# Three value products in other PSUM banks, the down unit's low parts last, and one weight split moved behind an addition

## The chip, the core and the metric

The kernel runs on one core of one Trainium2 chip. The metric is the device time of one execution in microseconds (us), the median of the runs shown. Matrix products run on TensorE (PE in the rows; PEld is its weight load), elementwise work on VectorE (DVE), ScalarE (ACT) and GpSimd (POOL), and transfers between the chip's memory and the core are started from SyncE's queue (SP), from POOL's and from ACT's.

## What is computed

One inference step of a two-layer decoder over 512 prompt tokens and 8 sample tokens (520 columns), with 1024 features. Layer 0 mixes tokens by sliding-window attention, layer 1 by gated linear attention (GLA). Behind each mixer comes a normalisation, then a gated feed-forward with a causal convolution, then another normalisation:

```python
def conv_ffn(x, buf, w_up, conv_w, conv_b, w_down):
    T = x.shape[1]
    h = x @ w_up
    a, u = h[..., :D_FF], h[..., D_FF:]          # gate branch, value branch; D_FF = 2816
    ap = jnp.concatenate([buf.astype(a.dtype), a], axis=1)
    c = conv_b + sum(conv_w[j] * ap[:, j:j + T] for j in range(CONV_W))
    y = (jax.nn.gelu(c, approximate=False) * u) @ w_down
    return y, ap[:, T:]
...
        xp = layer_norm(ALPHA * xp + mp, ln_mix_g[i], ln_mix_b[i])
        fp, cp = conv_ffn(xp, buf0, ffn_w_up[i], ffn_conv_w[i], ffn_conv_b[i], ffn_w_down[i])
        xp = layer_norm(ALPHA * xp + fp, ln_ffn_g[i], ln_ffn_b[i])
```

## The kernel before

All activations are held transposed, features on the 128 partitions and tokens along the row, in two groups of columns: group a has tokens 0 to 255, group b tokens 256 to 511 and the 8 sample tokens (264 columns). Every 32-bit operand of a matrix product is split into a high and a low part that TensorE reads in a single pass each. A product is then three matmuls for every 128 features: high weight by high input (L236), high weight by low input (L238) and low weight by high input (L240, or L243 where the lows come last). In the rows `xh`/`xl` are the high and low parts of the input, `wh`/`wl` those of a weight; `xs_a` and `hs_a` hold both parts of group a.

A weight is a tile of 128 x 1024, loaded into `raw` from SP's queue. ScalarE copies it to `wh` (L194, L313). The low part is made in one of two ways: VectorE subtracts (`wl<-raw,wh`, L200, L314), or ScalarE writes the negated high part to `wl` (L205) and a transfer from POOL's queue adds the weight from memory onto it (`low_by_dma`, L206). The up weights of the plain blocks, and those of the down units in `ffn_down2`, take the second way.

The first four of the 22 blocks of 128 feed-forward features are "plain": for each group a gate product (`ffn_gate`), then a value product (`ffn_value`), whose result VectorE multiplies by the gate (`hprod`, L817). I write g2a for the gate of block 2, group a, and v2a for its value. They begin while the normalisation of the mixer is still at work on group b. The products go into a ring of four PSUM banks named accp (`ACCS = 4`); the normalisation has banks of its own, `tp`, `pv` and two of `sc`, handed out by `mtile`. VectorE's eight `x_b<-x_b,par,pv` (L435) are the last to read the norm's `pv` for group b; behind them ScalarE makes `xh_b` (L436).

The other 18 blocks are "pairs" (`ffn_pair`): seven half products per block, in double banks widep0 to widep2 and two single ones (`onep`). ScalarE copies onep to `nv` (L852) and VectorE adds it to a wide bank (`merged<-widep,nv`, L844). Between the pairs stand down units. `ffn_down2` handles the first parts of the down product: for two column blocks s, and for each feature block, high-high, high-low and low-high (L919, L920, L921). The last part is `ffn_down`: four heads and four further products, each of which goes to `ln_chunk`, where VectorE adds it to x (L335) and TensorE forms a first sum of the norm from column block 0 (`sc<-x_a,ones_a`, L341). The weights of this last part are let loose (`release`) in a chosen order: `kinds` lists six of them.

The code is written in an order of tasks, but the order on each engine is set when the program is built: a list scheduler with its own estimates places every instruction, and then it is fixed. `issue_after(ins)` forbids placing an instruction ahead of another. So a change of three lines can move rows in stages whose code it doesn't touch.

Of the kernel before, what the change touches and what calls it, by code (L numbers as in the profile page):

```python
# [11 lines left out]
F32 = mybir.dt.float32  # L12
# [3 lines left out]
ALU = mybir.AluOpType  # L16
# [4 lines left out]
P = 128  # L21
# [64 lines left out]
def in_turn(rows):  # L86

    return rows.rearrange("p t j -> p j t")
# [10 lines left out]
class Net:  # L99
# [124 lines left out]
    def product(self, g, u, rh, rl):  # L224
        nc = self.nc
        h, l = self.w[u]
        nt = self.units[u][1]

        tail = u in self.phases[2::3] or g.i and u in self.phases[2:4]
        behind = self.units[u][2] == self.ffn_down and g.i == 0 or g.i == 0 and nt == KD and not tail and any(e < u < e + LOWS for e in (*self.phases[2:4], *self.phases[5:6]))  # L230
        ps = self.acc.tile([P, 512], F32, name="accp")
        o = ps[:, :g.n].rearrange("p (j t) -> p j t", t=2)
        for k in range(nt):
            ks = slice(k * P, (k + 1) * P)
            xh, xl = in_turn(rh[:, k]), in_turn(rl[:, k])
            nc.tensor.matmul(o, h[:, ks], xh, start=k == 0, stop=False)  # L236
            if not tail:
                nc.tensor.matmul(o, h[:, ks], xl, start=False, stop=False)  # L238
            if not behind:
                nc.tensor.matmul(o, l[:, ks], xh, start=False, stop=not tail and k == nt - 1)  # L240
        for k in range(nt) if tail or behind else ():
            w, r = (h, rl) if tail else (l, rh)
            nc.tensor.matmul(o, w[:, k * P:(k + 1) * P], in_turn(r[:, k]), start=False, stop=k == nt - 1)  # L243
        self.final = self.nc.cur_bb.bb.instructions[-1]
        return ps[:, :g.n]
# [80 lines left out]
    def ln_chunk(self, g, m, ps, scaled, last=False):  # L326


        nc, n, x = self.nc, g.n, g.x
        t = lambda name: self.ln.tile([P, g.n], F32, name=f"{name}_{g.name}")  # L330
        c = lambda name, b=1: self.ln.tile([P, NT - 256], F32, name=name, bufs=b)[:, :n]
        if m:
            yield 0
        if scaled:
            nc.vector.scalar_tensor_tensor(x[:, m], x[:, m], self.back[:, m:m + 1], ps, op0=ALU.add, op1=ALU.add)  # L335
        else:
            nc.vector.scalar_tensor_tensor(x[:, m], x[:, m], ALPHA, ps, op0=ALU.mult, op1=ALU.add)
        if m == 0:
            yield 1
            mp = self.mtile("sc")[:, :n]  # L340
            nc.tensor.matmul(mp, self.ones_a, x[:, 0], start=True, stop=True)  # L341
            sb = c("sb")
            nc.scalar.activation(sb, mp, AF.Copy, scale=float(KD))
            sa = sb
            if not scaled:
                sa = c("sa")
                nc.scalar.activation(sa, mp, AF.Copy, scale=KD / ALPHA)
            for i in range(KD):
                eng = nc.gpsimd if i else nc.vector
                eng.tensor_tensor(x[:, i], x[:, i], sa if i else sb, op=ALU.subtract)  # L350
            g.s2 = t("s2")
            nc.scalar.activation(g.s2, x[:, 0], AF.Square)
            return
        q = c("sq", 2)
        sq = nc.scalar.activation(q, x[:, m], AF.Square)
        if m == 6 and g.i == 0:
            with self.tc.issue_after(sq.ins):
                nc.scalar.preload_act_table_set("natural_log_exp_and_others")
        if last and m == KD - 1:

            g.q = q
            return
        if m == 1:
            g.s1 = t("s1")

        p1, p2 = (KD - 1, KD - 1) if g.i and not last else (0, S2P)
        (nc.gpsimd if m < p1 else nc.vector).tensor_tensor(g.s1, x[:, 0] if m == 1 else g.s1, x[:, m], op=ALU.add)
        (nc.gpsimd if m < p2 else nc.vector).tensor_tensor(g.s2, g.s2, q, op=ALU.add)
# [452 lines left out]
    def ffn_pair(self, u, layer, j, q):  # L821


        nc, W = self.nc, self.w[u]
# [18 lines left out]
        n, m = a.n, b.n  # L843
# [3 lines left out]
        g, h = M[:, 0], M[:, 1, 2:]  # L847
# [38 lines left out]
        if j == NF - 1:  # L886
            kinds, self.held = self.held, None
            done = [next(x for x in reversed(nc.cur_bb.bb.instructions) if x.engine == engine)
                    for engine in (mybir.EngineType.Activation, mybir.EngineType.DVE)]
            with self.tc.issue_after(summed.ins):  # L890
                self.release()
                self.release(kinds[0])
            with self.tc.issue_after(done[0]), self.tc.issue_after(done[1]):
                for kind in kinds[1:]:
                    self.release(kind)
            nc.scalar.dma_start(out=self.O["conv_p"][layer], in_=self.nconv_p)
            nc.scalar.dma_start(out=self.O["conv_s"][layer], in_=self.nconv_s)
            for cm in (self.cp_cm, self.pp_cm, self.fp_cm):
                self.close(cm)
            self.close_psum()  # L900
            self.open_acc()

    def ffn_down2(self, u, layer, part, i):


        nc = self.nc
        h, l = self.w[u]
        j0, j1 = FF_PARTS[part]
        nk = j1 - j0
        ms = KD // nk  # L910
        for g, m in ((g, ms * i + m) for g in self.groups for m in range(0, ms, 2)):
            ps, n = self.wide(), g.n
            for s in range(2):
                o = ps[:, s, :n].rearrange("p (j t) -> p j t", t=2)
                for k in range(nk):
                    t, q = (m % ms + s) * nk + k, self.place(j0 + k)
                    ks = slice(t * P, t * P + P)
                    rh, rl = in_turn(g.hh[:, q]), in_turn(g.hl[:, q])
                    nc.tensor.matmul(o, h[:, ks], rh, start=k == 0, stop=False)  # L919
                    nc.tensor.matmul(o, h[:, ks], rl, start=False, stop=False)  # L920
                    self.final = nc.tensor.matmul(o, l[:, ks], rh, start=False, stop=k == nk - 1).ins  # L921
            x = g.x[:, m:m + 2]
            if part == 0:
                nc.vector.scalar_tensor_tensor(x, x, ALPHA, ps[:, :, :n], op0=ALU.mult, op1=ALU.add)
            else:
                nc.vector.tensor_tensor(x, x, ps[:, :, :n], op=ALU.add)
        self.release()
# [565 lines left out]
```

## Time and profile before

| | us |
|---|---|
| median of three runs | 1099.32 |
| lowest, highest | 1099.08, 1100.93 |
| profiled execution | 1098.55 |
| its span, first to last instruction | 1096.6 |
| TensorE busy in it | 1058.9 (97%) |
| VectorE, ScalarE, POOL busy | 882.0, 663.1, 303.1 |
| mean granted TensorE clock | 0.994 of full speed |

In a row of the timeline the first number is the start in us from the span's start, the second how long it was busy; then engine, line, operation, output and inputs, and the count where equal instructions are gathered. In brackets stands the idle time ahead of it and what ended that. Matmuls overlap: at full clock one starts about every 112 ns though each is 280 long, so a gap is read from start to start. In a row of windows stand the stretch, its length, the busy time of PE, PEld, DVE, ACT and POOL with counts, the granted clock, the share of the transfer engines and GB/s.

The plain blocks of layer 0 lie at about 170 to 214 us, those of layer 1 at about 745 to 790; the pairs at 225 to 455 and 802 to 1035; the last down parts at about 470 and 1047; the GLA stage at 520 to 740.

### The profile page before, as it was taken

To read this page: it belongs to the slowest core of one execution; us is meant where nothing else is said; L and a number is where in the kernel's file an instruction comes from. 1 tells how busy PE (TensorE), PEld (TensorE's weight loads), DVE (VectorE), ACT (ScalarE), POOL (GpSimd) and SP (SyncE) were. 2 spreads that over 40 slices of the span, in tenths; PEclk is the share of its full clock that TensorE was granted. 3 is DMA by queue.
4 is the path that set the end of the run, shared out by engine and by line. 5 is a ranking of instruction groups with operands and counts; after the bars stand their busy time and mean duration, and the time that the engine had idled before them with its cause. 6 is when DMAs were issued, how large, how long until landed. Compare 5 with 4: busy or idle time off the path is not lost.

```text
span 1096.6 us, 23781 instructions
## 1 busy us (share of the span) xinstructions
PE 1058.9 (97%) x9174; PEld 1031.2 (94%) x9174; DVE 882.0 (80%) x1797; ACT 663.1 (60%) x1308; POOL 303.1 (28%) x512
## 2 busy tenths in 40 slices
PE   8999999999999999999899999999999999999996
PEld 8997899999999999999799899899999999999995
DVE  7897668988778878978667678778988788888975
ACT  5677667766655665547545456458776655655643
POOL 4576562221111110274111100362221111110163
PEclk9999999999999999999999999999999999999998
DMA  7554048587777774437224364558588777774412
GB/s 233 147 173 125 21 128 207 135 215 191 180 177 178 176 174 116 124 130 204 66 74 145 115 185 136 164 170 215 134 205 197 180 174 177 175 185 116 116 66 79
DMA packets 65472, 167.44 MB, mean 153 GB/s; under 512 B 8104, under 2 KB 28624, under 8 KB 65360
## 3 DMA queue, kind: packets, MB, share of 16 engines
q1 hardware_dynamic: 50960, 119.47, 33.8%
q0 software_dynamic: 12240, 44.57, 23.1%
q10 hardware_dynamic: 2160, 1.89, 0.5%
q8 instruction: 72, 1.18, 0.4%
q14 instruction: 40, 0.33, 0.1%
HBM read 153.24 MB, written 8.47 MB: 147 GB/s over the span
## 4 chain that ended last, share of the span: by engine, by line
PE 66%; DVE 13%; DMA 10%; ACT 5%; issue 5%; SPq 1%; POOL 0%; DVEq 0%; ACTq 0%; POOLq 0%
PE widep L308 8%; PE widep L310 8%; PE widep L309 8%; PE accp L236 6%; PE accp L238 6%; PE accp L240 6%; PE widep L921 5%; PE widep L920 5%; PE widep L919 5%; DMA vb<-dv 2%; DMA wl<-in_w_up 2%; DVE wl L200 2%; PE onep L310 1%; PE onep L309 1%; PE onep L308 1%
## 5 line engine op out<-in xcount | busy, mean ns | idle before, releaser
L313 ACT ACTIVATE wh<-raw 128x1024 fp32r<-128x1024 f32 x72 | 76.2, 1061 | 98.7 <-PE widep L920 57.3
L194 ACT ACTIVATE wh<-raw 128x1024 fp32r<-128x1024 f32 (+1 forms) x92 | 96.0, 1047 | 52.3 <-PE accp L238 19.4
L309 PE MATMUL widep<-tl,wh 128*128 128x264 f32 (+1 forms) x432 | 119.1, 276 | 0.0
L310 PE MATMUL widep<-th,wl 128*128 128x264 f32 (+1 forms) x432 | 119.1, 276 | 0.0
L308 PE MATMUL widep<-th,wh 128*128 128x264 f32 (+1 forms) x432 | 119.1, 276 | 0.0
L236 PE MATMUL accp<-xh_b,wh 128*128 128x264 f32 x400 | 113.1, 283 | 2.6 <-DVE hprod L817 2.6
L240 PE MATMUL accp<-xh_b,wl 128*128 128x264 f32 x400 | 111.5, 279 | 0.0
L236 PE MATMUL accp<-xs_a,wh 128*128 128x256 f32 x400 | 106.1, 285 | 5.4 <-DVE sg L1202 2.5
L238 PE MATMUL accp<-xl_b,wh 128*128 128x264 f32 x384 | 107.5, 280 | 0.0
L206 POOL DMA_DIRECT2D wl<-in_w_down x28 | 24.3, 866 | 293.6 <-ACT wl L205 271.0
L238 PE MATMUL accp<-xs_a,wh 128*128 128x256 f32 x384 | 103.1, 284 | 0.5
L314 DVE TENSOR_TENSOR wl<-raw,wh 128x1024 fp32r<-128x1024 f32 x72 | 87.5, 1218 | 7.5 <-ACT wh L313 7.5
L205 ACT ACTIVATE wl<-wh 128x1024 fp32r<-128x1024 f32 x85 | 89.1, 1051 | 1.0
L200 DVE TENSOR_TENSOR wl<-raw,wh 128x1024 fp32r<-128x1024 f32 (+2 forms) x64 | 79.0, 1244 | 12.3 <-ACT wh L194 11.5
L236 PEld LDWEIGHTS accp<-xs_a,wh 128*128 128x128 f32 x400 | 76.7, 195 | 7.0 <-DVE sg L1202 2.9
L308 PEld LDWEIGHTS widep<-th,wh 128*128 128x128 f32 x432 | 82.1, 190 | 0.0
L309 PEld LDWEIGHTS widep<-tl,wh 128*128 128x128 f32 x432 | 82.1, 190 | 0.0
L310 PEld LDWEIGHTS widep<-th,wl 128*128 128x128 f32 x432 | 82.1, 190 | 0.0
L236 PEld LDWEIGHTS accp<-xh_b,wh 128*128 128x128 f32 x400 | 75.7, 189 | 4.3 <-DVE hprod L817 3.4
L308 PE MATMUL widep<-xh_b,wh 128*128 128x264 f32 x288 | 79.6, 276 | 0.0
L309 PE MATMUL widep<-xl_b,wh 128*128 128x264 f32 x288 | 79.5, 276 | 0.0
L310 PE MATMUL widep<-xh_b,wl 128*128 128x264 f32 x288 | 79.5, 276 | 0.0
(419 smaller groups left out, 4113.1 us busy)
## 6 DMA issues: line engine op xcount, KB each, us to landing
raw<-in_w_up SPq DMA_DIRECT2D x88, 512.0 KB, 4.0
wl<-in_w_up POOLq DMA_DIRECT2D x52, 512.0 KB, 7.1
raw<-in_w_down SPq DMA_DIRECT2D x44, 512.0 KB, 3.9
wl<-in_w_down POOLq DMA_DIRECT2D x28, 512.0 KB, 6.5
raw<-in_w_gla SPq DMA_DIRECT2D x24, 512.0 KB, 3.5
raw<-in_w_mix_o SPq DMA_DIRECT2D x16, 512.0 KB, 4.1
qs<-hl SPq DMA_DIRECT2D x64, 64.0 KB, 2.1
sgla<-in_state_gla SPq DMA_DIRECT2D x16, 256.0 KB, 2.9
```

The costliest lines, as they stand in the source:

```text
L194: nc.scalar.activation(h[:, c], r[:, c], AF.Copy)
L200: nc.vector.tensor_tensor(l[:, c], r[:, c], h[:, c].bitcast(F32), op=ALU.subtract)
L205: self.nc.scalar.activation(l, h.bitcast(F32), AF.Copy, scale=-1.0)
L236: nc.tensor.matmul(o, h[:, ks], xh, start=k == 0, stop=False)
L238: nc.tensor.matmul(o, h[:, ks], xl, start=False, stop=False)
L240: nc.tensor.matmul(o, l[:, ks], xh, start=False, stop=not tail and k == nt - 1)
L308: self.nc.tensor.matmul(o, h[:, ks], rh, start=k == 0, stop=False)
L309: self.nc.tensor.matmul(o, h[:, ks], rl, start=False, stop=False)
L310: self.final = self.nc.tensor.matmul(o, l[:, ks], rh, start=False, stop=k == KD // 2 - 1).ins
L313: self.nc.scalar.activation(hi, src, AF.Copy)
L314: self.nc.vector.tensor_tensor(lo, src, hi.bitcast(F32), op=ALU.subtract)
L919: nc.tensor.matmul(o, h[:, ks], rh, start=k == 0, stop=False)
```

## The change

Three edits, A in `product`, B in `ffn_down2` and C in `ffn_pair` with `ln_chunk`:

- A: the value of block 1 for group b is accumulated in the norm's `tp` bank, that of block 2 for group a in `pv`, that of block 2 for group b in `sc`, where all three took a bank of the accp ring.
- B: in `ffn_down2` the high matmuls of both s come first and the low ones (L921) of both last, where each feature block had its low right behind its highs.
- C: of the six weights of the last down part, the sixth (`kinds[2:]`) is no longer released behind the last elementwise work of the last pair, but behind the first addition to x (`ln_chunk`, m = 0, group a).

```diff
-        ps = self.acc.tile([P, 512], F32, name="accp")
+        bank = self.units[u][2] == self.ffn_value and {(1, 1): "tp", (2, 0): "pv", (2, 1): "sc"}.get((self.units[u][3][1], g.i))
+        ps = self.mtile(bank) if bank else self.acc.tile([P, 512], F32, name="accp")
...
-            nc.vector.scalar_tensor_tensor(x[:, m], x[:, m], self.back[:, m:m + 1], ps, op0=ALU.add, op1=ALU.add)
+            first = nc.vector.scalar_tensor_tensor(x[:, m], x[:, m], self.back[:, m:m + 1], ps, op0=ALU.add, op1=ALU.add)
+            if m == 0 and g.i == 0:
+                with self.tc.issue_after(first.ins):
+                    for kind in self.kept:
+                        self.release(kind)
...
-                for kind in kinds[1:]:
-                    self.release(kind)
+                self.release(kinds[1])
+            self.kept = kinds[2:]
...
-            for s in range(2):
+            for low, s in ((0, 0), (0, 1), (1, 0), (1, 1)):
                 o = ps[:, s, :n].rearrange("p (j t) -> p j t", t=2)
                 for k in range(nk):
...
+                    if low:
+                        self.final = nc.tensor.matmul(o, l[:, ks], rh, start=False, stop=k == nk - 1).ins
+                        continue
                     nc.tensor.matmul(o, h[:, ks], rh, start=k == 0, stop=False)
                     nc.tensor.matmul(o, h[:, ks], rl, start=False, stop=False)
-                    self.final = nc.tensor.matmul(o, l[:, ks], rh, start=False, stop=k == nk - 1).ins
```

Lines of the changed kernel are higher by 1 (from 232), by 5 (from 336), by 8 (919 and 920) or 7 (from 922); L921 becomes 925.

What the scheduler makes of it, at four places. First TensorE's order in the plain blocks of layer 0, behind g2a (accp_2913). Numbers are those of tiles: 2947 is v2a, 2982 the gate of block 0 for group b (the first product that needs group b's normalised input), 3025 the gate of block 3 for group a, 3065 and 3175 the values of blocks 0 and 1 and 3246 that of block 2, all for group b. Before:

```order
L243 MATMUL accp_2913<-xs_a_87,wl_2626 128x256 x8
L236 MATMUL accp_2947<-xs_a_87,wh_2662 128x256
L238 MATMUL accp_2947<-xs_a_87,wh_2662 128x256
...
L238 MATMUL accp_2947<-xs_a_87,wh_2662 128x256
L243 MATMUL accp_2947<-xs_a_87,wl_2663 128x256 x8
L236 MATMUL accp_2982<-xh_b_90,wh_2405 128x264
L240 MATMUL accp_2982<-xh_b_90,wl_2406 128x264
L236 MATMUL accp_2982<-xh_b_90,wh_2405 128x264
L240 MATMUL accp_2982<-xh_b_90,wl_2406 128x264
L236 MATMUL accp_3025<-xs_a_87,wh_2749 128x256
```

After:

```order
L244 MATMUL accp_2913<-xs_a_87,wl_2626 128x256 x8
L237 MATMUL accp_2982<-xh_b_90,wh_2405 128x264
L241 MATMUL accp_2982<-xh_b_90,wl_2406 128x264
L237 MATMUL accp_3025<-xs_a_87,wh_2749 128x256
...
L239 MATMUL accp_3025<-xs_a_87,wh_2749 128x256
L237 MATMUL accp_3065<-xh_b_90,wh_2472 128x264
L237 MATMUL tp_3175<-xh_b_90,wh_2588 128x264
L237 MATMUL sc_3246<-xh_b_90,wh_2662 128x264
L237 MATMUL accp_2982<-xh_b_90,wh_2405 128x264
L241 MATMUL accp_2982<-xh_b_90,wl_2406 128x264
L244 MATMUL accp_3025<-xs_a_87,wl_2750 128x256 x8
...
L237 MATMUL pv_2947<-xs_a_87,wh_2662 128x256
```

The 24 rows' work of v2a stood between g2a and group b's first gate; now that gate and block 3's gate come straight behind g2a, the lows of block 3 (`wl_2750`) follow a few matmuls of group b, and v2a, in `pv`, comes after them. Layer 1 has the same order.

Second, the start of the first pair in layer 0, on ScalarE and on VectorE. `hh_b` are the high parts of the last two plain blocks, 3364 and 3428 the weights of the first pair, 3318 and 3328 low parts that a transfer completes (3318 that of the first down unit). ScalarE before, then after:

```order
L313 ACTIVATE wh3_3312<-sum3_3139 128x512
L271 ACTIVATE wh_3327<-raw_3323 128x1024
L205 ACTIVATE wl_3318<-wh_3317 128x1024
L852 COPY nv_3412<-onep_3399 128x256
L313 ACTIVATE hh_b_92<-hprod_3271 128x264
L313 ACTIVATE hh_b_92<-hprod_3357 128x264
L205 ACTIVATE wl_3328<-wh_3327 128x1024
L313 ACTIVATE wh_3364<-raw_3324 128x1024
L313 ACTIVATE wh_3428<-raw_3323 128x1024
```

```order
L314 ACTIVATE wh3_3312<-sum3_3139 128x512
L205 ACTIVATE wl_3318<-wh_3317 128x1024
L272 ACTIVATE wh_3327<-raw_3323 128x1024
L314 ACTIVATE hh_b_92<-hprod_3271 128x264
L314 ACTIVATE hh_b_92<-hprod_3357 128x264
L205 ACTIVATE wl_3328<-wh_3327 128x1024
L314 ACTIVATE wh_3364<-raw_3324 128x1024
L857 COPY nv_3412<-onep_3399 128x256
L314 ACTIVATE wh_3428<-raw_3323 128x1024
```

The copy that a transfer waits for (`wl_3318`) moved ahead of one weight copy, and `nv` moved behind two `hh_b`, a `wl` and a `wh` copy. VectorE before, then after:

```order
L314 TENSOR_TENSOR hl_b_93<-hprod_3357,hh_b_92 128x264
L259 TENSOR_TENSOR raw_3323<-raw_3323 128x512
L844 TENSOR_TENSOR merged0_3382<-widep0_3396,nv_3412 128x2x256
L314 TENSOR_TENSOR wl_3365<-raw_3324,wh_3364 128x1024
L314 TENSOR_TENSOR wl_3429<-raw_3323,wh_3428 128x1024
L844 TENSOR_TENSOR conv0_3384<-widep2_3398,merged0_3382 128x2x256
```

```order
L260 TENSOR_TENSOR raw_3323<-raw_3324,raw_3323 128x512
L260 TENSOR_TENSOR raw_3323<-raw_3323 128x512
L315 TENSOR_TENSOR wl_3365<-raw_3324,wh_3364 128x1024
L315 TENSOR_TENSOR wl_3429<-raw_3323,wh_3428 128x1024
L849 TENSOR_TENSOR merged0_3382<-widep0_3396,nv_3412 128x2x256
L849 TENSOR_TENSOR conv0_3384<-widep2_3398,merged0_3382 128x2x256
```

The addition that reads bank widep0 stood ahead of the two low splits of the first pair and now stands behind both.

Third, VectorE at the last down part of layer 0, before and after:

```order
L314 TENSOR_TENSOR hl_b_93<-merged1_3383,hh_b_92 128x264
L200 TENSOR_TENSOR wl_6619<-raw_6617,wh_6618 128x1024
L200 TENSOR_TENSOR wl_6625<-raw_6623,wh_6624 128x1024
L335 SCALAR_TENSOR_TENSOR x_a_86<-x_a_86,back_85,accp_6642 128x256
L350 TENSOR_TENSOR x_a_86<-x_a_86,sb_6739 128x256
```

```order
L315 TENSOR_TENSOR hl_b_93<-merged1_3383,hh_b_92 128x264
L200 TENSOR_TENSOR wl_6619<-raw_6617,wh_6618 128x1024
L336 SCALAR_TENSOR_TENSOR x_a_86<-x_a_86,back_85,accp_6636 128x256
L200 TENSOR_TENSOR wl_6730<-raw_6728,wh_6729 128x1024
L355 TENSOR_TENSOR x_a_86<-x_a_86,sb_6739 128x256
```

The addition to x stood behind two splits, now the second split stands behind it.

Fourth, VectorE in the GLA stage, at the gate product of the first head, `sg_7511`. Before, then after:

```order
L1034 COPY bl_7474<-dcum_7465 128x2
L1200 RECIPROCAL de_7507<-de_7507 128x256
L1117 COPY ebl_7303<-eb_7472 128x1
L1036 TENSOR_SCALAR dcum_7465<-dcum_7465,bl_7474 128x64 x2
L1116 TENSOR_TENSOR tst_7302<-sc_7557,sp_7561 128x256
L1025 TENSOR_SCALAR dmn_7611<-sc_7609,par_78 128x264
L200 TENSOR_TENSOR wl_7702<-raw_7700,wh_7701 128x1024
L1202 TENSOR_TENSOR sg_7511<-accp_7482,de_7507 128x256
```

```order
L1041 COPY bl_7474<-dcum_7465 128x2
L200 TENSOR_TENSOR wl_7665<-raw_7663,wh_7664 128x1024
L1116 COPY tst_7302<-sc_7552 128x256
L1043 TENSOR_SCALAR dcum_7465<-dcum_7465,bl_7474 128x64 x2
L1124 COPY ebl_7303<-eb_7472 128x1
L1207 RECIPROCAL de_7507<-de_7507 128x256
L1121 TENSOR_SCALAR sp_7561<-tst_7302,f_7559 128x256
L1209 TENSOR_TENSOR sg_7511<-accp_7482,de_7507 128x256
L1032 TENSOR_SCALAR dmn_7611<-sc_7609,par_78 128x264
L200 TENSOR_TENSOR wl_7702<-raw_7700,wh_7701 128x1024
L1123 TENSOR_TENSOR tst_7302<-sc_7557,sp_7561 128x256
```

The multiplication that reads the product's bank (`sg`) stood behind the split of `wl_7702`, and now stands ahead of it; another split, `wl_7665`, moved from ahead of this piece into it.

## The prediction, made before the changed kernel was run

> **What bounds the kernel now.** I read the page first: the busy shares, the chain that ended last, then the waits of TensorE by what they wait for, then the stages, and last the instructions around each place that the change touches.
>
> ```profile
> PE 1058.9 (97%) x9174; PEld 1031.2 (94%) x9174; DVE 882.0 (80%) x1797; ACT 663.1 (60%) x1308; POOL 303.1 (28%) x512
> PE 66%; DVE 13%; DMA 10%; ACT 5%; issue 5%; SPq 1%; POOL 0%; DVEq 0%; ACTq 0%; POOLq 0%
> 225.00:455.00 230.00, 230.00 (x2052) 230.00 (x2053) 190.25 (x323) 139.95 (x205) 32.22 (x63) 1.00 0.71 172
> 520.00:740.00 220.00, 211.60 (x1756) 200.97 (x1755) 162.39 (x383) 116.37 (x288) 45.39 (x68) 0.99 0.45 132
> 802.00:1035.00 233.00, 233.00 (x2081) 233.00 (x2079) 193.31 (x329) 140.12 (x206) 32.82 (x63) 1.00 0.70 171
> ```
>
> The last three rows are stretches of the span: the first number is their length, the second TensorE's busy time in them. In both pair stretches (225 to 455, 802 to 1035) TensorE never idles: 230.00 of 230.00. So a microsecond won or lost ahead of such a stretch is kept to its end, and only places where TensorE waits can give time. The change adds and removes no matmul. Its three parts stand in these rows of TensorE's waits (total, times, longest):
>
> ```profile
> PE accp L236 <- DVE hprod L817: 2.6, 4, 1.0
> PE sc L341 <- DVE x_a L335: 2.5, 2, 1.4
> PE widep L921 <- DMA wl<-in_w_down: 2.0, 2, 1.1
> PE accp L236 <- DVE sg L1202: 2.5, 1, 2.5
> ```
>
> The first is the ring of four accp banks (part A), the second the last down product's first sum (C), the third the low part in the first down unit (B). The fourth lies in the GLA stage, whose code is untouched but whose order moves. All prices below are against the profiled execution, 1098.55 us (span 1096.6 and 1.95 around it); the median of the runs, 1099.32, lies 0.77 above it, and I add that at the end. A change under 0.2% (2.2 us) can't be told from none here.
>
> **Part A, three values in the norm's banks.** TensorE in layer 0, then the three instructions elsewhere that matter (VectorE's eight x_b, ScalarE's first two xh_b, the issue of the low-weight transfer):
>
> ```profile
> 179.65 1.06 PE L243 MATMUL accp<-xs_a,wl 128*128 128x256 f32 x8
> 183.00 1.16 PE L243 MATMUL accp<-xs_a,wl 128*128 128x256 f32 x8 [0.51 <-DMA wl<-in_w_up]
> 188.33 0.94 PE L243 MATMUL accp<-xs_a,wl 128*128 128x256 f32 x6 [0.25 <-DMA wl<-in_w_up]
> 193.77 0.38 PE L236 MATMUL accp<-xh_b,wh 128*128 128x264 f32 x1 [0.91 <-DVE hprod L817]
> 182.04 3.28 DVE L435 SCALAR_TENSOR_TENSOR x_b<-x_b,par,pv 128x264 f32<-128x264 f32 x8
> 182.56 1.01 ACT L436 ACTIVATE xh_b<-x_b,par 128x264 fp32r<-128x264 f32 x2
> 179.57 0.86 POOL L206 DMA_DIRECT2D wl<-in_w_up  x1 [1.17 <-ACT wl L205]
> ```
>
> Before, the value of block 2 for group a (24 matmuls) runs from 180.55 to 184.00 and covers the time in which VectorE and ScalarE make group b's x_b and xh_b. In the new order it stands in the norm's pv bank, behind the eight x_b that read that bank (to 185.32), and comes 24 rows later. What follows g2a (the gate of block 2, which ends 180.55) is group b's first gate: it needs xh_b[0], ready at 182.56 plus half of 1.01, with the semaphore about 183.1. TensorE idles some 2.4 us. Then come 23 matmuls at 112.5 ns (from the spacing of rows above: eight in 0.90) to 185.7, and then the lows of block 3's gate, whose transfer was issued at 179.57 and let the old order continue at 188.33: a second idle of 2.6. The two waits at 183.00 and 188.33 (0.67 and 0.41 over the spacing) fall away in exchange: 2.4 + 2.6 - 1.1 = 3.9 us behind at 188.33. Counted in rows it is the same: there the new order has issued 35 matmuls fewer, 35 x 0.1125 = 3.9.
>
> A TensorE that is 3.9 us late no longer waits for banks and transfers behind it: the bank at 193.77 (1.07 over the spacing), another at 200.25 (0.52), a low at 203.54 (0.49), and a first step of 0.1 after each: 2.5. Net for layer 0: +1.4 us. A different bank could remove these waits without the idle; that is what the part offers, and I count it as the first rival.
>
> Layer 1 has the same rows:
>
> ```profile
> 757.21 1.06 PE L243 MATMUL accp<-xs_a,wl 128*128 128x256 f32 x8
> 759.22 1.02 ACT L436 ACTIVATE xh_b<-x_b,par 128x264 fp32r<-128x264 f32 x2
> wl<-in_w_up POOLq DMA_DIRECT2D x1, 512.0 KB, 8.2
> 770.46 0.38 PE L236 MATMUL accp<-xh_b,wh 128*128 128x264 f32 x1 [1.02 <-DVE hprod L817]
> ```
>
> g2a ends at 758.11, xh_b[0] is there at about 759.75: idle 1.6. 23 matmuls to 762.4, and the transfer (issued 756.23, 8.2 to landing) is there at 764.4: idle 2.0. 0.3 falls away, 3.4 us behind with the first steps; what is caught up is 1.19 (770.46), 0.53, 0.25 and their first steps, 2.5. Net +0.9. A is +2.3 in sum; its bounds are -5.0 (the 2.5 of each layer without an idle) and +7.3 (both idles and nothing caught up).
>
> **Part B, lows last in the first down unit.**
>
> ```profile
> 224.92 0.38 PE L921 MATMUL widep<-hs_a,wl 128*128 128x256 f32 x1 [0.92 <-DMA wl<-in_w_down]
> 801.57 0.38 PE L921 MATMUL widep<-hs_a,wl 128*128 128x256 f32 x1 [1.10 <-DMA wl<-in_w_down]
> 218.93 0.35 ACT L852 COPY nv<-onep 128x256 f32<-128x256 f32 x1
> 220.87 1.99 ACT L313 ACTIVATE wh<-raw 128x1024 fp32r<-128x1024 f32 x2
> 223.62 0.27 PE L919 MATMUL widep<-hs_a,wh 128*128 128x256 f32 x1
> 221.31 0.68 DVE L844 TENSOR_TENSOR merged<-widep,nv 128x512 f32<-128x512 f32 x1
> 221.94 2.36 DVE L314 TENSOR_TENSOR wl<-raw,wh 128x1024 fp32r<-128x1024 f32 x2
> ```
>
> The first low comes 14 matmuls (1.6 us) later than now, so the two waits (1.08 and 1.27 over the spacing) go. But the new order puts nv behind hh_b, a wl copy and a wh copy on ScalarE, and merged behind both wl splits on VectorE. The second split waits for the second wh copy (ends 222.86) and takes 1.2, merged 0.68 more: about 224.7, where it now ends at 221.99. Merged reads bank widep0, and w_down's first product, on TensorE at 223.62, is the next to write it: a new wait of some 1.1 us, in layer 1 by the same rows about 1.0 to 1.1. I take -0.2 for B in both layers; bounds -2.35 (no new wait) and +1 (both splits late by another half).
>
> **Part C, the sixth weight's split behind the first sum.**
>
> ```profile
> 469.75 2.36 DVE L200 TENSOR_TENSOR wl<-raw,wh 128x1024 fp32r<-128x1024 f32 x2 [0.50 <-ACT wh L194]
> 472.03 0.47 DVE L335 SCALAR_TENSOR_TENSOR x_a<-x_a,back,accp 128x256 f32<-128x256 f32 x1
> 472.56 0.70 PE L341 MATMUL sc<-x_a,ones_a 128*128 128x256 f32 x2 [1.41 <-DVE x_a L335]
> 1048.87 0.70 PE L341 MATMUL sc<-x_a,ones_a 128*128 128x256 f32 x2 [1.08 <-DVE x_a L335]
> ```
>
> TensorE has finished the sum's operand by 471.15 and waits for x_a, which stands behind two splits of 1.18. One of them now comes after it: x_a starts 1.14 earlier, at about 470.9, where its operand is just there. The same holds in layer 1, where the wait of 1.08 to 1.24 all but goes. Behind the add on VectorE nothing but the split is delayed, by 0.47; its weight serves the last two columns of the down product, over 2 us later on TensorE, and that is the cover. C is -2.25; bounds -2.5 (the whole row of waits) and -1 (one layer alone).
>
> **The GLA stage.** No line of it changes, yet several dozen rows of its order do. The largest wait of the whole trace is there:
>
> ```profile
> 540.03 0.59 PE L1118 MATMUL pv<-vk,attm 128*128 128x256 f32 x2
> 543.16 0.38 PE L236 MATMUL accp<-xs_a,wh 128*128 128x256 f32 x1 [2.53 <-DVE sg L1202]
> 541.56 1.21 DVE L200 TENSOR_TENSOR wl<-raw,wh 128x1024 fp32r<-128x1024 f32 x1
> 542.69 0.41 DVE L1202 TENSOR_TENSOR sg<-accp,de 128x256 f32<-128x256 f32 x1
> 543.88 0.42 PE L240 MATMUL accp<-xs_a,wl 128*128 128x256 f32 x1
> 543.20:547.20 4.00, 4.00 (x21) 4.00 (x22) 2.46 (x5) 1.53 (x6) 3.60 (x8) 0.57 0.43 131
> 547.20:551.20 4.00, 4.00 (x38) 4.00 (x38) 3.06 (x11) 2.21 (x7) 0.52 (x2) 1.00 0.00 0
> 607.75 0.33 PE L1090 MATMUL tp<-ident,k_b 128*128 128x128 f32 x1 [1.74 <-DVE sg L1210]
> 607.00:611.00 4.00, 3.25 (x27) 3.20 (x28) 2.74 (x7) 2.93 (x6) 0.00 (x0) 1.00 0.49 171
> ```
>
> In the new order sg comes ahead of that split of 1.21 and of two small operations. TensorE then resumes at least 1.2 earlier. After the wait the granted clock was 0.57 over four microseconds, with 21 matmuls where the next four have 38: some 15 matmuls cost 0.1 more each, 1.6 us. The wait at 607.75, 2.0 between starts, left the clock at 1.00, so with a gap of 1.7 that stretch may go too: -1.2 to -2.8, and I take the middle, -2.0. The rest of the reorder has no sign that I can read; TensorE idles 8.4 us of these 220 already, and +-3 is the bound.
>
> Here the Trainium skill has a rule (page "TensorE: Matmul & The Clock Gate", Part 1): the clock falls to half after an idle window of about 3.4 us, free-running. This trace fell to half after a gap of 2.9 between starts, so the measurement decides and the limit is lower than the Trainium skill has it. By the Trainium skill's rule the 2.4 and 2.6 of part A cost no clock, and the sum stays as it is; by the row at 543.88 they may, and that is the second rival.
>
> **Sum.** A +2.3, B -0.2, C -2.25, GLA -2.0: -2.15. 1098.55 - 2.15 = 1096.4 for the profiled execution, 1097.2 for the median.
>
> **Rivals.**
> - All waits simply go: A gives the 2.5 of each layer, because xh_b or the low-weight transfer comes earlier in the new program than now; with C's 2.25, B's 0.2 and the GLA's 2.0 that is -9.5, 1090; with A's rows of waits alone (2.6) about 1092.3. Against it: the copy that feeds xh_b has nothing moved ahead of it in the new order, and TensorE has nothing else to issue between g2a and group b's gate.
> - Slower, by the clock: the idle ahead of g3a's lows (2.6 and 2.0) trips the gate. The first idle's half clock would be hidden, since its 23 matmuls then only fill the second one. After the second, one half-clock window costs 15 x 0.1 = 1.6 per layer: 1100.4, no change. Two windows in a row in both layers cost 6.4: 1103.6. It decides above 4.3 us. For it: 2.9 was enough at 540; against it: 2.0 at 607.75 was not, and the second idles, 2.6 and 2.0 long, lie between the two.
> - The GLA reshuffle gives its gain back at another of its waits: the sum is -0.15, 1099.2, no change; with another wait of the size of 543.16 it would be slower, about 1101.7.
> - B's new wait doesn't come: 1095.
>
> **How the numbers follow.** Forecast (-0.5 to -4): 0.48, about half of it beyond the bound. Waits all go, or B's do: 0.13. Clock: 0.17, most of it slower. GLA gives back: 0.22, mostly within the bound. Faster 0.43, same 0.37, slower 0.20. The range leaves out one in ten on each side: from 1093.5 (B in full and half of the GLA's bound) to 1101.8 (the GLA's bad case). The likeliest case's own range is 1095 to 1098.8.
>
> **What the new profile would show.** A: TensorE idle behind g2a's lows, first for ScalarE's xh_b, then for a transfer of in_w_up, and no row of L236 (237) on hprod any more. If the two idles are missing, A is wrong; if TensorE's clock column shows less than 1.00 between 181 and 195, the second rival. B: no wait of the low line for in_w_down, but one of the high line for merged. C: the sc row's two waits together under 0.6 us, and the sixth weight's split behind x_a with nobody waiting for it. GLA: a gap under 2 us at 540 and no half clock behind it. It is wrong above all if the GLA stage's length moves by more than 3 us.

## The result and the profile after

The changed kernel takes 1105.92 us (median of 10 runs, 1101.4 to 1109.84), the kernel before 1099.81 beside it (10 runs, 1096.81 to 1102.19): ratio 1.005, 95% interval 1.0033 to 1.0066. It is slower by 0.5%, where 1097.2 with 1093.5 to 1101.8 was forecast. The profiled execution has a span of 1104.0, 7.4 more than before.

First the page's busy shares of the changed kernel, then its waits of TensorE (total, times, longest):

```profile
PE 1064.2 (96%) x9174; PEld 1036.0 (94%) x9174; DVE 882.9 (80%) x1797; ACT 666.9 (60%) x1308; POOL 306.3 (28%) x512
```

```profile
PE accp L244 <- DMA wl<-in_w_up: 4.4, 3, 2.4
PE accp L237 <- ACT xh_b L441: 2.8, 2, 2.0
PE onep L309 <- DVE hprod L822: 2.7, 1, 2.7
PE sc L655 <- ACT pr L672: 2.5, 6, 0.7
PE accp L237 <- ACT wh L194: 2.2, 3, 1.4
PE accp L237 <- ACT hh_b L314: 2.2, 2, 1.7
PE tp L1097 <- DVE sg L1217: 1.4, 1, 1.4
PE widep L927 <- ACT merged L863: 1.2, 1, 1.2
```

The work is the same (9174 matmuls, the same busy time of VectorE); what changed is who is waited for. The four waits that the prediction started from (accp for hprod, sc for x_a, the low of in_w_down, accp for sg) are gone or small. In their place stand three waits for transfers of in_w_up, two for xh_b, one of onep for hprod and one of widep for merged. The wait of onep is in no sentence of the prediction.

Since every version issues the same 9174 matmuls, the start of the n-th can be compared between traces. The table gives, for each stage, by how much TensorE fell behind (+) or caught up (-) against the profiled execution of before, in us. The stages end at matmul 1300, at the first pair product of layer 0 (1730), 400 later, at 4100 (behind the last sum of layer 0), 6000, 6200, at the first pair product of layer 1 (6586), 400 later, and at the last. A kernel's column is one execution; the row "ahead", where TensorE's order is alike in all, shows how far single executions differ without any cause in the code (the four columns with +1.5 or more have a stretch at half clock at about 136 us, the others don't). The last row has the median of all runs of the kernel less that of the kernel before beside it: the profiled executions of "no sc" and "sc" lie 3.6 and 3.4 above the medians of their kernels, that of B+C 2.8 below. The kernels of the other columns are told below.

| stage | change | B+C | A | no sc | swap | pv | sc | tp+B+C |
|---|---|---|---|---|---|---|---|---|
| ahead | +0.2 | -0.3 | +0.3 | +0.6 | +1.5 | +2.0 | +1.7 | +2.8 |
| plain blocks, layer 0 | +0.8 | -0.6 | +2.6 | +2.9 | +3.8 | +3.9 | +0.4 | -2.0 |
| first pairs and first down unit | +0.3 | -0.9 | +0.3 | -0.9 | -1.1 | 0.0 | +0.8 | -1.2 |
| pairs to the last down part | -1.5 | -0.9 | +0.1 | -1.5 | -1.2 | -0.3 | +0.1 | -1.1 |
| GLA stage | 0.0 | -1.2 | -0.6 | +3.1 | -2.4 | 0.0 | -2.1 | -0.5 |
| norm behind it | +1.9 | 0.0 | +2.1 | 0.0 | +1.9 | 0.0 | +2.1 | 0.0 |
| plain blocks, layer 1 | +6.8 | +0.2 | +5.3 | +4.8 | +2.8 | +4.1 | +3.5 | -0.3 |
| first pairs and first down unit | +0.1 | -1.3 | -1.3 | -1.4 | +0.7 | -0.3 | +0.4 | -1.4 |
| pairs to the end | -1.1 | -1.1 | 0.0 | -1.1 | -1.1 | 0.0 | 0.0 | -1.1 |
| sum | +7.4 | -6.1 | +8.9 | +6.5 | +4.9 | +9.3 | +6.8 | -4.6 |
| medians | +6.1 | -4.2 | +9.0 | +2.1 | +5.5 | +5.9 | +1.6 | -7.9 |

In the changed kernel 6.8 us are lost in one place, the plain blocks of layer 1; the other stages add up to +0.7. TensorE and VectorE there, in order of time, and the stretches with their granted clock:

```profile
759.82 1.16 PE L244 MATMUL accp<-xs_a,wl 128*128 128x256 f32 x8 [1.23 <-DMA wl<-in_w_up]
761.83 0.38 PE L237 MATMUL accp<-xh_b,wh 128*128 128x264 f32 x1 [0.85 <-ACT xh_b L441]
767.07 1.28 PE L244 MATMUL accp<-xs_a,wl 128*128 128x256 f32 x8 [2.40 <-DMA wl<-in_w_up]
796.08 0.28 PE L241 MATMUL accp<-xh_b,wl 128*128 128x264 f32 x1
799.09 0.55 PE L309 MATMUL onep<-xs_a,wh 128*128 128x256 f32 x1 [2.73 <-DVE hprod L822]
797.85 0.41 DVE L315 TENSOR_TENSOR xl_b<-mu,xh_b 128x256 fp32r<-128x256 f32 x1
798.52 0.42 DVE L822 TENSOR_TENSOR hprod<-conv,sc 128x264 f32<-128x264 f32 x1
```

```profile
768.00:772.00 4.00, 4.00 (x23) 4.00 (x23) 4.00 (x12) 0.91 (x4) 0.27 (x2) 0.58 0.00 0
796.00:800.00 4.00, 1.26 (x8) 1.10 (x7) 3.96 (x10) 4.00 (x9) 0.00 (x0) 0.84 0.45 142
800.00:804.00 4.00, 4.00 (x29) 4.00 (x28) 3.84 (x7) 4.00 (x7) 1.96 (x4) 0.74 0.86 208
```

The two forecast idles are there (761.83: 1.13 from start to start, 1.0 over the spacing; 767.07: 2.67 and 2.56). Behind the second the clock is 0.58 for four microseconds (23 matmuls instead of 38: 1.6 us). Then TensorE finishes the plain blocks at 796.08, and the first pair product can't begin until VectorE has read the value of block 2 out of the sc bank, at 798.94; that is a gap of 3.0, and the clock falls again behind it (0.84, 0.74: some 12 matmuls at 0.21 instead of 0.11, 1.3 us). By the program's allocation the norm's tile sc lies in bank 0 in layer 1, and bank 0 is that of the first onep; in layer 0 bank 0 is tp, whose value is read long before. No trace shows bank numbers, but layer 0 of the same execution bears it out: there VectorE's read of sc ended 2.76 after the first pair product's start, as late as in layer 1 after it could have started, and nobody waited.

```profile
215.16 0.27 PE L309 MATMUL onep<-xs_a,wh 128*128 128x256 f32 x1
217.50 0.42 DVE L822 TENSOR_TENSOR hprod<-conv,sc 128x264 f32<-128x264 f32 x1
```

The other three places, in layer 0:

```profile
182.91 0.38 PE L237 MATMUL accp<-xh_b,wh 128*128 128x264 f32 x1 [1.98 <-ACT xh_b L441]
184.28:187.69 3.41, 2.72 (x14) 2.42 (x12) 3.41 (x11) 2.35 (x6) 0.00 (x0) 0.50 0.55 114
187.75 1.16 PE L244 MATMUL accp<-xs_a,wl 128*128 128x256 f32 x8 [0.74 <-DMA wl<-in_w_up]
224.98 0.68 DVE L849 TENSOR_TENSOR merged<-widep,nv 128x512 f32<-128x512 f32 x1
225.97 0.38 PE L927 MATMUL widep<-hs_a,wh 128*128 128x256 f32 x1 [1.23 <-ACT merged L863]
471.83 0.47 DVE L336 SCALAR_TENSOR_TENSOR x_a<-x_a,back,accp 128x256 f32<-128x256 f32 x1
472.36 0.70 PE L346 MATMUL sc<-x_a,ones_a 128*128 128x256 f32 x2
```

The idle for xh_b is 2.25 from start to start, that for the transfer 1.17. Between them the clock is at half (0.50, the second row), which stretches the matmuls that lie there and leaves less to wait for the transfer. TensorE is 4.0 behind at matmul 1500 and has 0.95 left of it at the first pair product. The merged addition stands behind both splits, and w_down's first product waits for it, as the order said. The sum follows its addition by half a microsecond and nobody waits in brackets.

### The profile page after: what moved, and what is told of

It reads as the page before. It is cut to its first block, busy times and chain, and to the rows that moved or that the text cites. A ratio compares the mean times of both kernels' runs of the same rounds, so it can differ in the third digit from the quotient of the medians.

```text
span 1104.0 us, 23773 instructions
## 1 busy us (share of the span) xinstructions
PE 1064.2 (96%) x9174; PEld 1036.0 (94%) x9174; DVE 882.9 (80%) x1797; ACT 666.9 (60%) x1308; POOL 306.3 (28%) x512
## 4 chain that ended last, share of the span: by engine, by line
PE 67%; DVE 12%; DMA 11%; ACT 5%; issue 3%; POOL 1%; SPq 1%; DVEq 0%; ACTq 0%; POOLq 0%
PE widep L309 9%; PE widep L310 9%; PE widep L311 9%; PE accp L237 5%; PE accp L239 5%; PE widep L927 5%; PE widep L928 5%; PE widep L925 5%; PE accp L241 4%; DMA vb<-dv 3%; PE accp L945 2%; DMA wl<-in_w_up 2%; DMA raw<-in_w_up 1%; PE onep L309 1%; PE onep L311 1%
## 5 line engine op out<-in xcount | busy, mean ns | idle before, releaser
L237 PE MATMUL accp<-xh_b,wh 128*128 128x264 f32 x368 | 104.1, 285 | 3.3 <-ACT xh_b L441 2.8
L237 PE MATMUL accp<-xs_a,wh 128*128 128x256 f32 x384 | 102.1, 284 | 2.9 <-ACT wh L194 2.2
L241 PE MATMUL accp<-xh_b,wl 128*128 128x264 f32 x368 | 103.3, 282 | 0.0
L239 PE MATMUL accp<-xs_a,wh 128*128 128x256 f32 x368 | 99.4, 285 | 0.2
L239 PE MATMUL accp<-xl_b,wh 128*128 128x264 f32 x352 | 98.0, 279 | 0.0
L849 DVE TENSOR_TENSOR merged<-widep,conv 128x528 f32<-128x528 f32 x72 | 37.4, 561 | 56.6 <-PE widep L311 56.5
L237 PEld LDWEIGHTS accp<-xs_a,wh 128*128 128x128 f32 x384 | 73.8, 195 | 4.2 <-ACT wh L194 2.8
```

## The experiments

The theory after the result was this. Part A alone loses, and each of its banks in its own way: pv moves the cover out of the time in which xh_b is made (two idles a layer), sc lies under the first pair product of layer 1 and changes the scheduler's order behind it, tp costs nothing. The rivals were that B's or C's moved work takes part, and that the first pair product waits for late values whatever their bank.

### Without part A

```diff
-        bank = self.units[u][2] == self.ffn_value and {...}
-        ps = self.mtile(bank) if bank else self.acc.tile([P, 512], F32, name="accp")
+        ps = self.acc.tile([P, 512], F32, name="accp")
```

> The change without part A (all three values back in the accp ring). Theory 1, the loss is part A alone: the plain blocks and the GLA stage are as before, C saves 1.3 in each layer, B about nothing: 2.6 less than before, about 1097.2 us. Rival, the loss lies in B's later nv and merged or in C's moved split: as slow as the whole change, 1103 or more.

Measured: 1095.15 us (8 runs), before 1099.37 beside it, ratio 0.9961 (0.9944 to 0.9978). The loss is part A's; B and C together gain 0.4%, which is 2 us more than expected, since B gains too. In the table B gives 0.9 and 1.3 in the first pairs and C 0.9 and 1.1 at the last down parts. Its waits have no row for in_w_down or merged; the four for the ring stay:

```profile
PE accp L236 <- DVE hprod L821: 2.0, 4, 0.8
```

### Part A alone

The two other edits undone.

> Part A alone. Theory 1: layer 0's plain blocks +0.8, GLA stage +1.4 by its changed order, layer 1's plain blocks and the wait of the first pair product +7.2 and a half-clock stretch behind it +1.2: 10.6 more than before, about 1110.4 us, with the wait of onep for hprod of 2.5 to 3 us in layer 1. Rival, B or C take part in the loss: at most 6 more than before.

Measured: 1108.33 us (6 runs), ratio 1.0093 (1.0072 to 1.0114), 8.9 in the profiled execution. The theory's figure was 1.7 too high: layer 1 lost less than expected (no half clock came behind the wait of onep), layer 0 more. B and C have no part in the loss. The two largest of its new waits:

```profile
PE accp L244 <- DMA wl<-in_w_up: 5.1, 3, 2.9
PE onep L309 <- DVE hprod L818: 2.7, 1, 2.7
```

### The change without the sc bank

```diff
-{(1, 1): "tp", (2, 0): "pv", (2, 1): "sc"}
+{(1, 1): "tp", (2, 0): "pv"}
```

> The whole change but the value of block 2 for group b stays in the accp ring; tp and pv are used as in the change. Theory 1 (the first pair product of layer 1 waits because its bank 0 is the sc bank of that value): the wait of onep for hprod and the half clock behind it go, 4.4 us; the order of the GLA stage stays as before (its rows differ in 20 places, not 185), 1.4 less; the two idles in each layer stay: about 1099.5 to 1100.5 us. Rival, late products whatever their bank: onep still waits for hprod, 1104 or more.

Measured: 1101.45 us (12 runs), ratio 1.0016 (0.9998 to 1.0035), not to be told from before, 0.3% below the whole change by the two ratios and 1 us above the expected range. In its trace the GLA stage, whose order is nearly that of before, lost 3.1: it has two stretches at half clock where before has one, and its time, 1105.04, is the third longest of the twelve. No wait of onep is left, and merged stands ahead of the splits again. The idles stay, and now they are all that is lost in the plain blocks: 2.9 in layer 0, 4.8 in layer 1, with the clock at half behind the second idle.

```profile
183.51 0.38 PE L237 MATMUL accp<-xh_b,wh 128*128 128x264 f32 x1 [2.19 <-ACT xh_b L441]
763.77 0.38 PE L237 MATMUL accp<-xh_b,wh 128*128 128x264 f32 x1 [1.16 <-ACT xh_b L441]
769.31 2.08 PE L244 MATMUL accp<-xs_a,wl 128*128 128x256 f32 x8 [2.81 <-DMA wl<-in_w_up]
770.00:774.00 4.00, 4.00 (x21) 4.00 (x21) 3.98 (x12) 0.93 (x4) 0.34 (x2) 0.50 0.00 0
```

### The banks tp and sc exchanged

```diff
-{(1, 1): "tp", (2, 0): "pv", (2, 1): "sc"}
+{(1, 1): "sc", (2, 0): "pv", (2, 1): "tp"}
```

> The whole change with two banks exchanged: the value of block 1 for group b in sc, that of block 2 in tp; the order of all engines stays as in the change but for 4 places. In layer 1 sc is bank 0 (the first pair product's) and tp bank 2 (widep0's, needed 12 matmuls later). Theory 1: onep no longer waits; widep0 waits 1.3 to 1.5 for the same hprod, and the clock stays full: 1.5 to 2.8 less than the change, 1103.2 to 1104.5 us. Rival, the wait is not of the bank: onep still waits 2.7, 1106 us.

Measured: 1104.82 us (6 runs), ratio 1.0055 (1.0037 to 1.0074). The time is 0.3 above the expected range, but that it came so near was luck: the expectation had no wait in layer 0, and the wait of onep went there from layer 1.

```profile
219.54 0.35 PE L309 MATMUL onep<-xs_a,wh 128*128 128x256 f32 x1 [2.73 <-DVE hprod L822]
218.97 0.42 DVE L822 TENSOR_TENSOR hprod<-conv,tp 128x264 f32<-128x264 f32 x1
798.84 0.35 PE L309 MATMUL widep<-xs_a,wh 128*128 128x256 f32 x1 [1.39 <-DVE hprod L822]
798.27 0.42 DVE L822 TENSOR_TENSOR hprod<-conv,tp 128x264 f32<-128x264 f32 x1
```

In layer 0 tp is bank 0, so now the value of block 2 lies under the first onep there; in layer 1 tp is bank 2, that of widep0, 12 matmuls later, and the wait is 1.4. VectorE's order differs from the change's in four places only, ScalarE's in none. VectorE's read of the value of block 2 ends about 2.75 us after the first pair product starts or could start, in both layers of both kernels. So the wait goes with the bank, not with the lateness of the value.

### pv alone

Of part A only `{(2, 0): "pv"}`; neither B nor C.

> Of part A only the value of block 2 for group a goes to pv; no B, no C. The order of the GLA stage and of the first pair stays as before. Theory 1 (pv costs by the two idles that the lost cover leaves in each layer, and by a half clock behind the second): +0.8 to +2.9 in layer 0, +4 to +5 in layer 1, no wait of onep for hprod: 5 to 8 more than before, 1104.5 to 1107.5 us. Rival, the idles are made good by the bank waits behind them: within 1.5 of before.

Measured: 1106.1 us (4 runs), before 1100.18 beside it, ratio 1.0056 (1.0043 to 1.007). The order of the GLA stage and of the pairs is that of before, and the stages between the plain blocks are within 0.4 of it. The idles cost 3.9 in layer 0, more than expected, and 4.1 in layer 1, each with a half clock behind the second one; what they save behind them doesn't pay for it.

```profile
185.04 0.38 PE L237 MATMUL accp<-xh_b,wh 128*128 128x264 f32 x1 [2.32 <-ACT xh_b L437]
189.97 1.55 PE L244 MATMUL accp<-xs_a,wl 128*128 128x256 f32 x8 [2.31 <-DMA wl<-in_w_up]
770.24 1.55 PE L244 MATMUL accp<-xs_a,wl 128*128 128x256 f32 x8 [2.74 <-DMA wl<-in_w_up]
770.20:774.20 4.00, 3.96 (x21) 3.96 (x22) 4.00 (x14) 0.06 (x1) 0.00 (x0) 0.58 0.00 0
```

### sc alone

Of part A only `{(2, 1): "sc"}`; neither B nor C.

> Of part A only the value of block 2 for group b goes to sc; no B, no C. The cover behind the gate of block 2 stays, so no idle of over 1 us at 181 and 760. Theory 1 (sc costs by the bank it shares with the first pair product of layer 1, by the late merged, and by the changed GLA order): onep waits about 1.5 to 2 in layer 1, merged is waited for about 1.2, the GLA stage and the norm behind it +1 to +2: 1101 to 1104 us. Rival, onep only waits when TensorE comes late from the idles: no wait of onep, 1100 to 1101.5 us.

Measured: 1101.73 us (9 runs, 1097.82 to 1109.01), ratio 1.0018 (0.9998 to 1.0038). The cover is back and no idle for xh_b is left (there are idles for transfers, 2.1 in layer 0, 1.4 and 1.5 in layer 1, which were not expected); yet onep waits, for longer than expected, and TensorE waits for merged too, without B:

```profile
PE onep L309 <- DVE hprod L818: 2.8, 1, 2.8
PE widep L920 <- ACT merged L859: 1.7, 1, 1.7
```

So the lateness of TensorE isn't needed for the wait, and the late merged comes from sc and not from B (part A alone has that wait too, 1.2). In the table the norm behind the GLA stage loses 2.1, while the GLA stage gains 2.1. As a time the run is inconclusive: the interval holds one. So sc's wait is shown by the traces, and its price in the median of all runs is not.

### tp alone with B and C

```diff
-{(1, 1): "tp", (2, 0): "pv", (2, 1): "sc"}
+{(1, 1): "tp"}
```

> B and C with only the value of block 1 for group b in tp, the candidate to beat both kernels. Theory 1: tp frees the ring without moving the cover or sharing the first pair product's bank at a bad time, so the accp wait for hprod of 0.8 to 1.0 goes in each layer: 1 to 2 below B and C alone (1095.15), 1093 to 1094.5 us. Rival, TensorE then only comes earlier to the next wait in the plain blocks: 1095 to 1096 us.

Measured: 1092.32 us (5 runs, 1090.26 to 1093.73), before 1100.18 beside it, ratio 0.9928 (0.9915 to 0.994). It is faster than both kernels, and 0.7 below the expected range. The ring's wait for hprod is gone from its waits; what is left in the plain blocks is transfers, of which three:

```profile
185.89 1.16 PE L244 MATMUL accp<-xs_a,wl 128*128 128x256 f32 x8 [0.55 <-DMA wl<-in_w_up]
205.53 0.38 PE L241 MATMUL accp<-xs_a,wl 128*128 128x256 f32 x1 [0.84 <-DMA wl<-in_w_up]
760.16 1.16 PE L244 MATMUL accp<-xs_a,wl 128*128 128x256 f32 x8 [1.10 <-DMA wl<-in_w_up]
```

### B alone, C alone, tp alone

Three short ones, each the kernel before with one edit.

> Part B alone. The order of nv and merged in the first pair is that of before. Theory 1 (the late merged came from sc, not from B): both waits of the low matmul for in_w_down go and nothing replaces them, 0.9 to 1.3 in each layer, about 1097 us. Rival (as predicted: B moves nv and merged): a wait of widep for merged of about 1.1 in each layer, 1099 us.

One execution: 1098.92 us, no time to judge by. Its trace has the two waits for in_w_down gone, 0.8 and 0.9 less in the two stages, and no wait of that size in their place:

```profile
PE widep L922 <- ACT merged L858: 0.2, 1, 0.2
```

> Part C alone. Theory 1: the two waits of sc for x_a (1.4 and 1.1) go, 1.1 to 1.5 less in each layer between the last pair and the last down part, nothing else moves: 2.3 to 2.6 less than before, about 1097.3 us. Rival, the split behind the addition is late for its products: a wait of accp for wl (L200) of about 1 takes the place, 1099.5 us.

Measured: 1097.69 us (10 runs), before 1098.57, ratio 0.9991 (0.9977 to 1.0006): inconclusive as a time. In the trace the two stages are 1.2 and 1.15 shorter, and of the wait is left

```profile
PE sc L345 <- DVE x_a L335: 0.3, 1, 0.3
```

with none for the moved split. The 2.3 expected (0.9979) is inside the interval, near its end.

> Of part A only the value of block 1 for group b goes to tp; no B, no C. Theory 1: tp alone carries what part A has to gain, 2 to 3 less than before (the 2.8 between 1092.32 and 1095.15), about 1097 to 1098 us, no wait of accp for hprod above 0.5. Rival, tp gains only together with B's earlier transfer: within 1 of before, 1099 to 1100.5 us.

Measured: 1096.77 us (10 runs, before 1098.57), ratio 0.9991 (0.9977 to 1.0006). The plain blocks of layer 0 are 2.5 shorter in its trace, but layer 1's only 0.2, and the norm behind the GLA stage is 1.8 longer. Which of the two expectations holds can't be said from this. The medians of tp, B and C one by one lie 1.8, 1.3 (one run) and 0.9 below before, that of all three at once 7.9; whether more than scatter is in that difference is open.

## Why the prediction was wrong

**The step that failed is part A's "Layer 1 has the same rows ... Net +0.9".** The stage lost 6.8. Of that 2.9 is the wait of onep for hprod, for which the sum had no term and no rival: it carried layer 0's banks over to layer 1 and never asked what lies under the first pair product there. In layer 1 that is sc. The half clock behind this wait costs another 1.3, which the table has in its next row. Then 1.6 is the half clock behind the second idle, and 2.3 are the idles themselves, where 0.9 was forecast; the exchanged kernel, which has neither half clock nor a wait of onep in layer 1, lost 2.8 there. The bound of A (+7.3) was for both layers' idles. The exchange of the two banks, which moves the wait to the other layer, and sc alone, which has it without the idles for xh_b, show the bank. Forecast and profiled execution are 9.6 apart: 5.9 is this stage, 3.9 the GLA stage with the norm behind it (below), and the rest nearly cancels.

**The clock.** The second rival, that the idle ahead of block 3's lows trips the gate, came true in layer 1 (0.58 for four microseconds, 1.6). In layer 0 that idle was 1.17 instead of 2.6, and it was the first idle that tripped it (0.50 from 184.28 to 187.69). As the rival said of that case, this was hidden: the slowed matmuls only filled the second idle. The price per window was right; the chance was too low: with pv alone both layers had a half clock behind the second idle.

**The idles themselves.** Layer 0: 2.25 and 1.17 where 2.4 and 2.6 were forecast. The half clock between them took 1.2 out of the second, and the transfer let TensorE go on at 187.75, not 188.33; this last is why the net is +0.8 and not +1.4. The three executions with a half clock behind the second idle lost 2.6, 2.9 and 3.9 in layer 0; the exchanged kernel, without one, 0.9 ahead of its wait of onep. Layer 1: 1.0 and 2.56 against 1.6 and 2.0, and a wait of 1.23 ahead of them for the lows of block 2's gate, whose transfer landed late; such waits stand also in kernels without pv or sc (0.82 with B and C alone, 0.96 and 1.10 with tp). The waits that the prediction names as caught up add to 2.4 and 2.3 with their first steps; its 2.5 has in it a small one each, at 196.93 and 773.62, that it doesn't name.

**The GLA stage.** The place that was priced did what was said: the largest gap at 540 is 0.46 instead of 2.9, sg comes at 541.16 ahead of the split, and no half clock follows. From matmul 4100 to 5900 the four kernels with sc gained 1.7 to 3.9. Then they lost 3.4 to 3.7 up to matmul 6200, where the other four of the table have -0.3; it begins behind matmul 5993 with a wait for `hh_b`, 1.8 to 1.9 from start to start in all four. In the changed kernel:

```profile
718.82 0.49 PE L237 MATMUL accp<-hh_b,wh 128*128 128x264 f32 x2 [1.67 <-ACT hh_b L314]
```

So the third rival, that the reshuffle gives its gain back at another of its waits, came true. With the half clock behind 528 (below) the balance of the two rows is +1.9 where -2.0 was taken, 3.9 apart and more than the +-3 that stood beside it; the other kernels with sc have +1.5, -0.5 and 0.0. Betting the middle of a gain on one visible wait of a reshuffled stage was a mistake of method.

**Part B.** The new wait for merged in layer 0 was right (1.23, +0.3 net against -0.1). In layer 1 merged stands behind both splits too, but the pair itself began 3.0 late, and nobody waits for it. The prediction laid the reorder to B. B alone and B with C keep merged ahead of the splits and gain 0.8 to 1.3 in each layer; the order moves with sc.

**Part C.** Forecast -2.25 for both layers, measured -1.5 and -1.1; the other kernels that have C show -0.9 to -1.5 and -1.1. Its cover held: no product waits for the moved split.

The rival "all waits simply go" was closest to what the parts can do: tp with B and C is 7.9 us below before.

## What to carry to other kernels

A bank or buffer that is lent to another use has a next owner: ask for each layer or repetition, not once, who allocates over it and when that owner starts, since the allocation may lie differently the second time. Ahead of moving a product behind a buffer's last reader, ask what that product was covering; 24 matmuls that look free were the cover of a norm, and the idle they left cost a second time through the clock. And where a list scheduler sets the order, build each edit alone and read its order before laying a moved row to one of them.

## What the runs showed of the clock

The length of an idle doesn't decide alone whether the clock falls. A gap of 1.8 from start to start at the same place of the GLA stage was followed by a lower clock in the changed kernel (first row) and not before (second row). One of 2.67 in the changed kernel was (the next two rows); one of 3.15 in the exchanged kernel was not (the last four):

```profile
528.00:532.00 4.00, 4.00 (x23) 4.00 (x24) 1.84 (x3) 0.52 (x2) 0.00 (x0) 0.63 0.41 124
528.20:532.20 4.00, 4.00 (x36) 4.00 (x37) 1.80 (x3) 0.49 (x2) 0.00 (x0) 1.00 0.40 125
764.55:767.96 3.41, 1.01 (x10) 0.90 (x9) 3.41 (x12) 1.07 (x3) 0.00 (x0) 1.00 0.40 90
767.96:771.37 3.41, 3.41 (x18) 3.41 (x17) 3.41 (x12) 0.28 (x1) 0.10 (x1) 0.50 0.00 0
189.20 1.05 PE L244 MATMUL accp<-xs_a,wl 128*128 128x256 f32 x7 [2.88 <-DMA wl<-in_w_up]
183.90:187.31 3.41, 2.42 (x22) 2.22 (x20) 3.41 (x10) 3.37 (x8) 0.19 (x1) 1.00 1.02 251
187.31:190.73 3.42, 1.53 (x13) 1.53 (x14) 3.42 (x11) 0.00 (x0) 0.00 (x0) 1.00 0.07 18
190.73:194.14 3.41, 3.41 (x33) 3.41 (x32) 3.41 (x12) 0.92 (x4) 0.37 (x2) 1.00 0.00 0
```

The traces show what else decides: where the idle falls on a grid. Within a trace the stretches at half clock last 3.41 us (or twice that) and begin whole multiples of 3.413 us apart; in the changed kernel they begin at 184.28, 529.03, 720.18, 767.96 and 798.68, which is 101, 56, 14 and 9 steps. From one execution to the next the grid lies elsewhere. I divided all twelve traces from 150 to 1080 us into the slices of their grids and counted 0.12 us of work for each matmul, so the idle times are estimates. All 15 slices with over 2.4 us of idle were followed by half clock, 8 of the 17 with 2.0 to 2.4, and none of those with less (a slice that was itself at half clock left out). The idle of the 2.67 lies within one slice but for 0.04; that of the 3.15 falls into two, with 1.2 and 1.9. So one and the same gap can trip the clock in one execution and not in another.

The Trainium skill (page "TensorE: Matmul & The Clock Gate", Part 1) says that the window in which activity is judged runs freely and doesn't reset when the kernel starts; the grid, which lies elsewhere in each execution, agrees with that. Its figure, an idle window of about 3.4 us, does not: 2.4 us in a slice were always enough here. A stretch of half clock costs 11 to 16 matmuls at 0.21 us instead of 0.11, that is 1.1 to 1.6 us, and nothing where it only fills an idle to come. Whether kernels with such idles spread more from run to run isn't shown: sc alone spreads over 11.2 us, but pv alone over 2.8 (4 runs) and tp with B and C over 3.5 (5 runs).
